# A load-bound log-sum-exp: an earlier Ln, one load fewer, and a first load issued as two partition halves from two queues

## The chip, the core and the metric

The kernel runs on one core of a Trainium2 chip. The time is device microseconds of that core, the median of several executions; single executions of the kernel before lie between 164.04 and 164.73 us over all sessions of this study.

## The reference

The input `x` has 32 x 512 rows of 1,024 float32 values (67.1 MB). The output is one float32 per row:

```python
x_max = np.max(x, axis=axis, keepdims=True)
return x_max.squeeze(axis) + np.log(np.sum(np.exp(x - x_max), axis=axis))
```

The kernel leaves out the maximum: it takes exp, sums, and takes the log. Each of the 128 SBUF partitions holds 128 rows.

## The kernel before

The 128 rows of each partition come in 18 loads ("chunks") into a ring of 51 row slots. ScalarE takes the exponential. In each chunk the first `n_dve` rows get one wide exponential and VectorE sums them; each other row gets an exponential of its own that also accumulates its sum. One Ln is taken early, over the rows of finished chunks, and one at the very end.

```python
CHUNKS = [   # (rows, rows summed by VectorE)
    (4, 0), (16, 10), (14, 13), (15, 4), (16, 7), (15, 6), (12, 9), (9, 6), (7, 5), (5, 4),
    (4, 3), (3, 3), (2, 2), (2, 0), (1, 1), (1, 0), (1, 0), (1, 0),
]
...
    def load(i):
        ...   # waits until the slots are free
        nc.sync.dma_start(out=ring[:, s : s + r], in_=x_v[:, row : row + r]).then_inc(
            landed[i], 16
        )
...
        if i == len(CHUNKS) - LN_EARLY:      # LN_EARLY = 6
            logged = place[i - 1][1]
            take_logs(0, logged, *done_before[i - 1])
        nc.scalar.wait_ge(landed[i], 16)
```

The first load is moved ahead of the barrier that opens the program, so that it is issued at 0.00 us of the profiled span. All loads are issued by SyncE and cover all 128 partitions.

The softmax here doesn't subtract the row's maximum and nothing guards it: scores larger than these inputs give would overflow.

Of the kernel before, what the change touches and what calls it, by code (L numbers as in the profile page):

```python
# [1 line left out]

# [4 lines left out]



CHUNKS = [  # L10
    (4, 0), (16, 10), (14, 13), (15, 4), (16, 7), (15, 6), (12, 9), (9, 6), (7, 5), (5, 4),
    (4, 3), (3, 3), (2, 2), (2, 0), (1, 1), (1, 0), (1, 0), (1, 0),
]
RING_ROWS = 51

LN_EARLY = 6


@with_exitstack
def kernel(  # L20
    ctx: ExitStack,
    tc: tile.TileContext,
    x: bass.AP,
    axis: bass.AP,
    out: bass.AP,
):
    nc = tc.nc
    P = nc.NUM_PARTITIONS

    assert axis in (-1, len(x.shape) - 1), f"only last-axis reduction supported, got {axis}"  # L30

    x_flat = x.flatten_outer_dims()
    N, D = x_flat.shape
    assert N % P == 0
    NB = N // P
    assert sum(r for r, _ in CHUNKS) == NB

    fp32 = mybir.dt.float32
    Exp = mybir.ActivationFunctionType.Exp
    Ln = mybir.ActivationFunctionType.Ln  # L40
    AX = mybir.AxisListType.X

    x_v = x_flat.rearrange("(p t) d -> p t d", p=P)
    out_v = bass.AP(tensor=out.tensor, offset=out.offset, ap=[[NB, P], [1, NB]])

    ring = nc.alloc_sbuf_tensor("ring", [P, RING_ROWS, D], fp32).ap()
    sums = nc.alloc_sbuf_tensor("sums", [P, NB], fp32).ap()
    res = nc.alloc_sbuf_tensor("res", [P, NB], fp32).ap()

    landed = [tc.alloc_semaphore(f"landed{i}") for i in range(len(CHUNKS))]  # L50
    act_done = tc.alloc_semaphore("act_done")
    dve_done = tc.alloc_semaphore("dve_done")
    stored = tc.alloc_semaphore("stored")


    hook = nc.pop_inst_callback()
    symbolic, nc._always_lower_symbolic_ap = nc._always_lower_symbolic_ap, False


    place = []  # L60
    row = slot = 0
    for r, _ in CHUNKS:
        if slot + r > RING_ROWS:
            slot = 0
        place.append((slot, row))
        slot += r
        row += r



    busy = [(0, 0)] * RING_ROWS
    acts = dves = 0

    def load(i):
        (s, row), r = place[i], CHUNKS[i][0]
        act_wait = max(a for a, _ in busy[s : s + r])
        dve_wait = max(d for _, d in busy[s : s + r])
        if dve_wait:
            nc.sync.wait_ge(dve_done, dve_wait)
        if act_wait:  # L80
            nc.sync.wait_ge(act_done, act_wait)
        nc.sync.dma_start(out=ring[:, s : s + r], in_=x_v[:, row : row + r]).then_inc(  # L82
            landed[i], 16
        )

    def take_logs(lo, hi, dve_wait, act_wait):
        nonlocal acts
        nc.scalar.wait_ge(act_done, act_wait)
        nc.scalar.wait_ge(dve_done, dve_wait)  # L89
        nc.scalar.activation(out=res[:, lo:hi], in_=sums[:, lo:hi], func=Ln).then_inc(  # L90
            act_done, 1
        )
        acts += 1

    body = nc.main_func.blocks[-1]
    assert not body.instructions
    load(0)
    n_early = len(body.instructions)

    nc.scalar.preload_act_table_set("natural_log_exp_and_others")  # L100

    logged = 0
    done_before = [(0, 0)]
    for i, (r, n_dve) in enumerate(CHUNKS):
        if i:
            load(i)
        s, row = place[i]
        if i == len(CHUNKS) - LN_EARLY:
            logged = place[i - 1][1]
            take_logs(0, logged, *done_before[i - 1])  # L110
        nc.scalar.wait_ge(landed[i], 16)
        if n_dve:
            nc.scalar.activation(  # L113
                out=ring[:, s : s + n_dve], in_=ring[:, s : s + n_dve], func=Exp
            ).then_inc(act_done, 1)
            acts += 1
            nc.vector.wait_ge(act_done, acts)
            nc.vector.reduce_sum(  # L118
                out=sums[:, row : row + n_dve], in_=ring[:, s : s + n_dve], axis=AX
            ).then_inc(dve_done, 1)  # L120
            dves += 1
            for j in range(n_dve):
                busy[s + j] = (0, dves)
        for j in range(n_dve, r):
            nc.scalar.activation(  # L125
                out=ring[:, s + j],
                in_=ring[:, s + j],
                func=Exp,
                accum_out=sums[:, row + j : row + j + 1],
            ).then_inc(act_done, 1)  # L130
            acts += 1
            busy[s + j] = (acts, 0)
        done_before.append((dves, acts))

    take_logs(logged, NB, dves, acts)
    nc.scalar.wait_ge(act_done, acts)
    nc.scalar.dma_start(out=out_v, in_=res).then_inc(stored, 16)
    nc.gpsimd.wait_ge(stored, 16)



    sp = mybir.EngineType.SP
    first = nc.main_func.blocks[0]
    head, work = first.instructions, body.instructions
    at = next(k for k, i in enumerate(head) if i.engine == sp and i.opcode == "Drain")
    end = next(k for k, i in enumerate(head) if i.opcode == "UnconditionalBranch")
    first.instructions = head[:at] + work[:n_early] + head[at:end] + work[n_early:] + head[end:]
    body.instructions = []

    nc._always_lower_symbolic_ap = symbolic  # L150
    nc.push_inst_callback(hook)


# [1 line left out]
_INS = ['x', 'axis']  # L155
_OUTS = [((32, 512), 'float32')]

_NUMBERS = {'axis': -1}


# [26 lines left out]
```

## Time and profile before

| | kernel before |
|---|---|
| time, median of 3 runs | 164.24 us (164.04 to 164.56) |
| span of the profiled execution | 162.7 us |
| load queue's share of the 16 DMA engines' time | 96.1% |
| ScalarE, VectorE busy | 76%, 49% |
| first chunk landed | 7.48 us |
| last chunk landed | 158.51 us |
| last exponential starts | 158.78 us |

The landings are read from the semaphore records: they show sixteen increments for a load, at separate times, and the sixteenth is the landing. The packet records give the start, duration and size of each piece that an engine moves; in the first load a packet is 16 KB, the four rows of one partition. They carry the queue but not the engine: where this text speaks of one engine's packets, each is taken to start where that engine's last one ended. The lines themselves stand in the prediction below, with what they show: the transfers never pause (the load queue fills 96.1% of the engines' time), and the end is the last landing at 158.51 us plus a short tail on ScalarE.

### The profile page before, as it was taken

How to read it: one execution, taken by the hardware profiler on the slowest of the kernel's cores; microseconds unless marked ns; L12 is line 12 of the kernel's file. 1: busy time of each engine (PE TensorE's matmuls, PEld its weight loads, DVE VectorE, ACT ScalarE, POOL GpSimd, SP SyncE). 2: the span in 40 equal slices, each digit the busy share in tenths (PEclk: the TensorE clock that was granted, in tenths of full speed). 3: DMA queues.
4: the chain of work that ended last, by engine and by line, in shares of the span. 5: the costliest groups of instructions: out<-in, count | busy, mean ns of one | idle time of the engine just before them, and what ended most of it. 6: DMA issues, size and time to landing. Idle time of an engine off the chain costs nothing.

```text
span 162.7 us, 208 instructions
## 1 busy us (share of the span) xinstructions
DVE 79.2 (49%) x13; ACT 123.2 (76%) x126; POOL 0.2 (0%) x4
## 2 busy tenths in 40 slices
DVE  0000000029940499990003940194009999999980
ACT  3180004999599707999099984999999999999893
POOL 0000000000000000000000000000000000000000
DMA  7997999989999979989997998998999999999960
GB/s 262 511 515 306 467 515 437 409 352 409 439 483 483 468 321 451 515 354 421 499 468 332 408 483 387 435 507 362 426 435 415 430 423 432 420 420 422 405 268 16
DMA packets 2737, 67.18 MB, mean 413 GB/s; under 512 B 304, under 2 KB 432, under 8 KB 944
## 3 DMA queue, kind: packets, MB, share of 16 engines
q1 hardware_dynamic: 2592, 67.11, 96.1%
q10 hardware_dynamic: 144, 0.07, 0.1%
q14 instruction: 1, 0.01, 0.0%
HBM read 67.11 MB, written 0.07 MB: 413 GB/s over the span
## 4 chain that ended last, share of the span: by engine, by line
DMA 45%; DVE 27%; ACT 26%; issue 0%; SPq 0%; ACTq 0%
DMA ring<-in_x_dram 45%; DVE sums L118 27%; ACT ring L113 17%; ACT ring L125 9%; ACT res L90 0%; SPq L82 0%; ACTq L89 0%
## 5 line engine op out<-in xcount | busy, mean ns | idle before, releaser
L118 DVE TENSOR_REDUCE sums<-ring 128x4 f32<-128x4096 f32 (+9 forms) x13 | 79.2, 6138 | 79.0 <-ACT ring L113 79.0
L113 ACT ACTIVATE ring<-ring 128x4096 f32<-128x4096 f32 (+9 forms) x13 | 64.8, 4987 | 30.3 <-DMA ring<-in_x_dram 30.2
L125 ACT ACTIVATE ring<-ring 128x1024 f32<-128x1024 f32 x55 | 57.2, 1040 | 5.5 <-DMA ring<-in_x_dram 5.5
L125 ACT ACTIVATION_READ_ACCUMULATOR ring<-ring 128x1 f32 x55 | 10.3, 187 | 0.0
L100 ACT ACT_TABLE_LOAD x1 | 1.3, 1283 | 0.8 <-PEq L168 0.8
L90 ACT ACTIVATE res<-sums 128x117 f32<-128x117 f32 (+1 forms) x2 | 0.5, 256 | 0.4 <-DVE sums L118 0.4
L168 POOL MEMSET const-bfloat16-1.0<- 128x1 bf16 x1 | 0.1, 102 | 0.0
L168 POOL MEMSET const-uint8-127<- 128x1 uint8 x1 | 0.1, 102 | 0.0
L168 POOL MEMSET const-float32-0.0<- 128x1 f32 x1 | 0.1, 99 | 0.2 <-issue 0.2
L168 POOL MEMSET const-float32-1.0<- 128x1 f32 x1 | 0.1, 99 | 0.0
## 6 DMA issues: line engine op xcount, KB each, us to landing
ring<-in_x_dram SPq DMA_DIRECT2D x2, 7680.0 KB, 45.3
ring<-in_x_dram SPq DMA_DIRECT2D x1, 7168.0 KB, 42.6
ring<-in_x_dram SPq DMA_DIRECT2D x1, 6144.0 KB, 40.9
ring<-in_x_dram SPq DMA_DIRECT2D x1, 4608.0 KB, 29.7
ring<-in_x_dram SPq DMA_DIRECT2D x2, 2048.0 KB, 20.0
ring<-in_x_dram SPq DMA_DIRECT2D x1, 3584.0 KB, 36.5
ring<-in_x_dram SPq DMA_DIRECT2D x1, 2560.0 KB, 28.1
ring<-in_x_dram SPq DMA_DIRECT2D x2, 1024.0 KB, 29.4
```

The lines of the kernel that those rows point to most:

```text
L90: nc.scalar.activation(out=res[:, lo:hi], in_=sums[:, lo:hi], func=Ln).then_inc(act_done, 1)
L100: nc.scalar.preload_act_table_set("natural_log_exp_and_others")
L113: nc.scalar.activation(out=ring[:, s : s + n_dve], in_=ring[:, s : s + n_dve], func=Exp).then_inc(act_done, 1)
L118: nc.vector.reduce_sum(out=sums[:, row : row + n_dve], in_=ring[:, s : s + n_dve], axis=AX).then_inc(dve_done, 1)
L125: nc.scalar.activation(out=ring[:, s + j], in_=ring[:, s + j], func=Exp, accum_out=sums[:, row + j : row + j + 1],).then_inc(act_done, 1)
L168: nc = _bacc.Bacc("TRN2", target_bir_lowering=False, num_devices=1)
```

## The change

The intent is to take the early Ln and its wait out of the tail, to save one load, and to have the DMA engines started sooner by handing the first load to two queues at once.

```diff
 CHUNKS = [
-    (4, 0), (16, 10), (14, 13), (15, 4), (16, 7), (15, 6), (12, 9), (9, 6), (7, 5), (5, 4),
-    (4, 3), (3, 3), (2, 2), (2, 0), (1, 1), (1, 0), (1, 0), (1, 0),
+    (4, 1), (15, 11), (16, 10), (16, 15), (16, 0), (14, 0), (12, 9), (9, 5), (7, 5), (5, 4),
+    (4, 3), (3, 0), (2, 2), (2, 2), (1, 0), (1, 0), (1, 0),
 ]
-LN_EARLY = 6
+LN_AT = 5
+FIRST_PARTS = [("sync", 0, 64), ("scalar", 64, 128)]
...
-        nc.sync.dma_start(out=ring[:, s : s + r], in_=x_v[:, row : row + r]).then_inc(
-            landed[i], 16
-        )
+        for engine, lo, hi in FIRST_PARTS if i == 0 else [("sync", 0, P)]:
+            getattr(nc, engine).dma_start(
+                out=ring[lo:hi, s : s + r], in_=x_v[lo:hi, row : row + r]
+            ).then_inc(landed[i], 16)
...
-        if i == len(CHUNKS) - LN_EARLY:
-            logged = place[i - 1][1]
-            take_logs(0, logged, *done_before[i - 1])
-        nc.scalar.wait_ge(landed[i], 16)
+        if i == LN_AT:
+            logged = row
+            take_logs(0, logged, *done_before[i])
+        nc.scalar.wait_ge(landed[i], 16 * (len(FIRST_PARTS) if i == 0 else 1))
```

The rest of the diff (cut) puts each early load ahead of its own engine's part of the opening barrier.

More of the change, by code (lines that the diff above doesn't have):

```diff
@@ L138 @@
     nc.gpsimd.wait_ge(stored, 16)
-    sp = mybir.EngineType.SP
     first = nc.main_func.blocks[0]
     head, work = first.instructions, body.instructions
-    at = next(k for k, i in enumerate(head) if i.engine == sp and i.opcode == "Drain")
     end = next(k for k, i in enumerate(head) if i.opcode == "UnconditionalBranch")
-    first.instructions = head[:at] + work[:n_early] + head[at:end] + work[n_early:] + head[end:]
+    head, tail = head[:end], head[end:]
+    for ins in work[:n_early]:
+        at = next(
+            k for k, i in enumerate(head) if i.engine == ins.engine and i.opcode == "Drain"
+        )
+        head.insert(at, ins)
+    first.instructions = head + work[n_early:] + tail
     body.instructions = []
```

## The prediction

Of the first rival, which the text goes on to call "a collision", only the size is left: each packet of a half load takes twice its 0.611 us, which makes +4.9 us and 169.

The 186 + 15 x 853 ns for an exponential of 15 rows agrees with the traces: 1,040 ns for one row and 11,296 for 13 in the kernel before make about 185 + 855 a row.

> **What bounds the kernel now.** I read the page first: the span, the DMA row of the 40 slices, the queue's share, and the chain that ended last.
>
> ```profile
> span 162.7 us, 208 instructions
> ...
> DMA  7997999989999979989997998998999999999960
> ...
> q1 hardware_dynamic: 2592, 67.11, 96.1%
> ...
> DMA 45%; DVE 27%; ACT 26%; issue 0%; SPq 0%; ACTq 0%
> ```
>
> The reader is to see that the one load queue fills 96.1% of the time of 16 DMA engines over the span, and that VectorE (49%) and ScalarE (76%) are not full. The chain names three causes in turn, but it follows buffer releases: the load queue always held the next load before the last one had landed (the fifth load was issued at 46.4 us while the fourth landed at 61.9). So the transfers never pause, and time is: start of the first packet, plus bytes at the engines' pace, plus what follows the last landing.
>
> The second view is the windows of the first microseconds (duration, DVE, ACT, POOL, clock, DMA share, GB/s).
>
> ```profile
> 1.00:1.50 0.50, 0.00 (x0) 0.50 (x1) 0.00 (x0) 1.00 0.70 164
> 1.50:2.00 0.50, 0.00 (x0) 0.50 (x1) 0.00 (x0) 1.00 1.01 295
> 2.00:2.50 0.50, 0.00 (x0) 0.06 (x1) 0.00 (x0) 1.00 0.62 262
> 2.50:3.00 0.50, 0.00 (x0) 0.00 (x0) 0.00 (x0) 1.00 1.07 459
> ```
>
> The load is issued at 0.0 and reaches its pace only after 2.5 us. The packet records beneath say why: the 16 engines take up their first packets between 1.00 and 2.01 us, and that first packet of 16 KB takes 0.61 to 1.51 us, where each later one takes 0.611. The engines end their eight packets at 6.35 to 7.12 us; without stagger and slow first packets it would be 1.00 + 8 x 0.611 = 5.9. The lag of one engine behind another then stays to the end, because each has the same bytes to move.
>
> The third view is the end: the windows of the DMA, and the timeline of ScalarE.
>
> ```profile
> 156.00:157.00 1.00, 1.00 (x2) 1.00 (x2) 0.00 (x0) 1.00 1.04 414
> 157.00:158.00 1.00, 1.00 (x2) 1.00 (x3) 0.00 (x0) 1.00 0.29 115
> 158.00:159.00 1.00, 0.15 (x1) 1.00 (x3) 0.00 (x0) 1.00 0.00 0
> ```
> ```profile
> 148.51 2.75 ACT L113 ACTIVATE ring<-ring 128x3072 f32<-128x3072 f32 x1
> 151.67 0.30 ACT L90 ACTIVATE res<-sums 128x117 f32<-128x117 f32 x1 [0.41 <-DVE sums L118]
> 151.88 1.89 ACT L113 ACTIVATE ring<-ring 128x2048 f32<-128x2048 f32 x1
> ...
> 156.70 1.04 ACT L125 ACTIVATE ring<-ring 128x1024 f32<-128x1024 f32 x1
> ...
> 157.74 1.04 ACT L125 ACTIVATE ring<-ring 128x1024 f32<-128x1024 f32 x1
> ...
> 158.78 1.04 ACT L125 ACTIVATE ring<-ring 128x1024 f32<-128x1024 f32 x1
> ...
> 159.94 0.21 ACT L90 ACTIVATE res<-sums 128x11 f32<-128x11 f32 x1
> 160.18 0.37 ACTq L137 DMA_DIRECT2D out_dram<-res  x1
> ```
>
> Data stop at 158.1; the last load's sixteen semaphore increments come from 157.40 to 158.51. The last exponential starts at 158.78, 0.27 after the last increment, because ScalarE runs without a gap from 151.67 on: it waited 0.41 us for VectorE before the early Ln and then spent some 0.2 on it. So the tail is bound by ScalarE, by a quarter of a microsecond.
>
> [...]
>
> **The change, part by part.**
>
> *17 loads.* From the packet records, by bytes per partition: 4 KB 161 ns, 60 KB 2267, 64 KB 2418, 56 KB 2116; eight of each per engine and load. The new list differs by one 64 KB load more, one 60 KB and one 4 KB load fewer: 8 x (2418 - 2267 - 161) = -80 ns, and a 9 ns semaphore write less: **-0.09 us** on the last landing.
>
> *Does the ring still feed the queue?* Rows 4 + 15 + 16 + 16 fill the 51 slots, so four loads go out at once, landing (pace 18.15 us per 15 rows, 19.35 per 16) at about 7.5, 25.6, 45.0 and 64.3. The tightest reload is the seventh, which needs VectorE's 15-row sum of the fourth chunk. The exponential starts at 64.3 and takes 186 + 15 x 853 ns = 13.0; the sum runs at 1.08 us per row (14.02 for 13 rows), 16.2. It ends at 93.5, while the sixth load lands at about 101. A margin of some 7 us; the fifth and sixth reloads have 17 and 19. ScalarE alone frees the later slots. No starvation: **0**.
>
> *Early Ln at the fifth chunk index.* It now logs 67 rows and needs the fourth chunk's sum (93.5), which is long done when ScalarE reaches it near 100.8 after 16 exponentials with accumulation (1.04 each). It costs about 0.3 us there, just as the sixth chunk lands, and later slack absorbs it. At the end both the 0.41 wait and the Ln are gone. I carried ScalarE's chain forward with pitches from the timeline (1.04 a row; 0.85 n + 0.09 for n rows) against landings shifted by the -0.09. It starts chunk seven at 115.65 (landed 115.60) and is never over 0.8 late; the longer 3-row chunk with accumulation, and two chunks of 2 rows, put the last exponential at about 158.6, against 158.78 before, just behind the landing at about 158.45. VectorE ends its last sum at 159.4, before the last Ln at 159.75. The last Ln has 61 columns instead of 11, +0.04. Net: **-0.15 us**, with the -0.09 inside it.
>
> *The first load in two halves.* SyncE and ScalarE each issue 64 partitions from 0.0 and about 0.1 us. ScalarE's arrival at the barrier comes after its own issue (0.37 us) and drain; the barrier was at 0.58, so it may be 0.1 later, harmless: the next load has until 6.3 us to be issued, and the table load (1.28 us) until the first landing. If the stagger of the first packets comes from feeding 128 descriptors through one queue, two half lists could cut it by up to half, 0.5 us. If it is the memory's first accesses, nothing. I take **-0.25 us**, and this is a choice, not a measurement; ScalarE's later starts move with the landings, so it would all reach the end.
>
> Sum: 164.24 - 0.15 - 0.25 = 163.84; I say **163.8**.
>
> **The rivals.**
> [...] the 2 MB would take 9.8 us instead of 4.9 (estimate: 8 packets x 0.611, doubled): +4.9 us, 169, slower by 3%. [...]
> *The start does not shorten.* [...] only -0.15 remains, 164.1.
> *ScalarE or VectorE takes over the end.* One of the chunks (3, 0), (2, 2), (2, 2) leaves a backlog. My margin for VectorE's last sum is 0.35 us. If it fails, the gain of the tail is lost: 164.0 to 164.4. Nothing could make it more, as the chain is full only by tenths.
> *An instruction fetch.* At 73.3 us an 8 KB fetch held one engine, which stays 0.43 behind the next one to the end. In the new kernel it may hit an engine with more or less lead: plus or minus 0.3.
>
> **Range and chances.** Without a collision I expect 163.2 to 164.3, from the start's 0 to -0.6 and the fetch. I give a collision of over a microsecond one chance in eight, which stretches the top: range 163.0 to 164.9. Faster by over 2% would need -3.3 us, where at most 1.2 is to be had at the start and 0.3 at the end: 0.01. Slower by over 2% needs most of the full collision: 0.07. The rest, 0.92, is within 2%.
>
> **What would show it.** Right: last landing at about 158.2, last exponential within 0.2 after it, no wait on VectorE before either Ln, load queue still near 96%, first packets of the engines begun within some 0.5 us, first chunk landed near 7.2 (or one big packet later, harmlessly, if an engine alternates with the second load). Wrong: 16 KB packets longer than 0.611 us after the ramp (the collision); an empty stretch of the DMA near 100 us (reload late); a wait for VectorE at the last Ln.

## The result

The changed kernel takes 169.75 us (median of 6 runs, 169.05 to 170.64), against 164.28 us for the kernel before in the same rounds. The ratio is 1.0337 (95% interval 1.0304 to 1.037). A ratio here is the mean time of one kernel's fast runs over that of the other's in the same rounds, so it is not quite the ratio of the two medians. The change made the kernel slower by 3.4%, and the time is outside the predicted range. The profiled execution of the changed kernel took 170.29 us, that of the kernel before 164.53; both are a little above their medians.

The page of the changed kernel, the same lines as in the prediction and the row of GB/s below the DMA row:

```profile
span 168.5 us, 214 instructions
...
DMA  8999699979997999699969999998999999999970
GB/s 187 260 354 339 292 467 467 467 342 436 498 451 311 482 498 451 296 498 498 451 296 436 438 436 436 502 420 385 440 429 429 417 436 397 428 425 419 412 311 16
...
q1 hardware_dynamic: 2384, 66.06, 93.7%
q10 hardware_dynamic: 224, 1.11, 2.8%
```

The row of GB/s of the kernel before:

```profile
GB/s 262 511 515 306 467 515 437 409 352 409 439 483 483 468 321 451 515 354 421 499 468 332 408 483 387 435 507 362 426 435 415 430 423 432 420 420 422 405 268 16
```

The DMA row does not tell that anything is wrong: the engines are as busy as before (the queues' lines sum to 96.5% of their time, to 96.2% before). The GB/s row does. A slice is about 4.2 us; the first five slices carry 187, 260, 354, 339 and 292 where the kernel before had 262, 511, 515, 306 and 467. (Large packets are counted where they start, so single slices jump up and down: before, 1,131 GB/s from 6 to 7 us and none from 10 to 11. Only sums over several mean something.) From the sixth slice on both are at the same pace. Two windows make it sharper; the columns are the window, its length, DVE, ACT and POOL busy, clock, DMA busy share, GB/s. Kernel before:

```profile
2.50:4.50 2.00, 0.00 (x0) 0.00 (x0) 0.00 (x0) 1.00 1.02 434
```

Changed kernel:

```profile
2.50:4.50 2.00, 0.00 (x0) 0.26 (x1) 0.00 (x0) 1.00 1.09 246
11.00:15.00 4.00, 0.00 (x0) 0.00 (x0) 0.00 (x0) 1.00 1.03 311
```

With the DMA share at 1.02 to 1.09 in all three, the changed kernel moves 246 GB/s in place of 434 in the middle of its first load, and still 311 when the second load is under way. The packet records agree: the median of the 16 KB packets that start between 2.8 and 4.5 us is 0.611 us before and 1.27 us after. The first half of the first chunk has landed at 8.72 us and the second at 20.68, where the whole chunk was in at 7.48 before.

Where the 5.8 us of the span come from can be added up. I sum, over the packets of the first load, what each took beyond 0.611 us, and divide by 16 engines: 0.40 us per engine before, 4.33 after, so +3.9. I do the same for the 60 KB packets of the second load, whose usual time is 2.267 us: 48 of them, three for each engine, took 2.4 to 3.6 us, which is +2.0 per engine; no packet of the second load before (64 KB, usually 2.418) took more than 2.47. That makes +6.0. The measured last landing is 164.41 in place of 158.51, +5.90.

The tail got shorter, as intended:

```profile
164.53 1.04 ACT L128 ACTIVATE ring<-ring 128x1024 f32<-128x1024 f32 x1
165.48 0.19 ACT L128 ACTIVATION_READ_ACCUMULATOR ring<-ring 128x1 f32 x1
165.69 0.25 ACT L93 ACTIVATE res<-sums 128x61 f32<-128x61 f32 x1
165.98 0.36 ACTq L140 DMA_DIRECT2D out_dram<-res  x1
```

These are ScalarE's last lines in the timeline of the changed kernel. The last exponential starts 0.12 us after the last landing, where it was 0.27 before.

### The profile page after: what moved, and what is told of

Same layout as the page of the kernel before. It is cut to its first block, busy times and chain, and to the rows that moved or that the text cites. A ratio compares the mean times of both kernels' runs of the same rounds, so it can differ in the third digit from the quotient of the medians.

```text
span 168.5 us, 214 instructions
## 1 busy us (share of the span) xinstructions
DVE 72.9 (43%) x11; ACT 124.0 (74%) x136; POOL 0.2 (0%) x4
## 4 chain that ended last, share of the span: by engine, by line
ACT 50%; DMA 40%; DVE 7%; issue 1%
DMA ring<-in_x_dram 40%; ACT ring L128 28%; ACT ring L116 21%; DVE sums L121 7%; ACT res L93 0%
## 5 line engine op out<-in xcount | busy, mean ns | idle before, releaser
L121 DVE TENSOR_REDUCE sums<-ring 128x5 f32<-128x5120 f32 (+8 forms) x11 | 72.9, 6648 | 92.3 <-ACT ring L116 92.2
L116 ACT ACTIVATE ring<-ring 128x5120 f32<-128x5120 f32 (+8 forms) x11 | 59.3, 5393 | 35.1 <-DMA ring<-in_x_dram 35.1
L128 ACT ACTIVATE ring<-ring 128x1024 f32<-128x1024 f32 x61 | 63.4, 1040 | 5.3 <-DMA ring<-in_x_dram 5.3
L128 ACT ACTIVATION_READ_ACCUMULATOR ring<-ring 128x1 f32 x61 | 11.4, 187 | 0.0
L93 ACT ACTIVATE res<-sums 128x67 f32<-128x67 f32 (+1 forms) x2 | 0.5, 256 | 0.1
```

The lines of the kernel that those rows point to most:

```text
L93: nc.scalar.activation(out=res[:, lo:hi], in_=sums[:, lo:hi], func=Ln).then_inc(act_done, 1)
L116: nc.scalar.activation(out=ring[:, s : s + n_dve], in_=ring[:, s : s + n_dve], func=Exp).then_inc(act_done, 1)
L121: nc.vector.reduce_sum(out=sums[:, row : row + n_dve], in_=ring[:, s : s + n_dve], axis=AX).then_inc(dve_done, 1)
L128: nc.scalar.activation(out=ring[:, s + j], in_=ring[:, s + j], func=Exp, accum_out=sums[:, row + j : row + j + 1],).then_inc(act_done, 1)
```

## The experiments

**The theories.** The partition theory: what counts is the set of partitions that a transfer writes; one that covers partitions 0 to 63 alone (or 64 to 127 alone) keeps all 16 DMA engines busy, but each of its packets takes about twice as long, as in the changed kernel (1.27 us for 0.611). In the expectations what stands after "[...]" is what this theory expects. Rival A: the chunk list or the place of the Ln costs the time. Rival B: the second queue costs, by taking turns or by its issue. Rival C: any transfer of fewer than 128 partitions is slow. Rival D: it is the half of the input in memory that is read, not what is written.

Eight kernels were run. The runs of the kernel before had a median of 164.57 us in the session of the first four and 164.21 us in that of the other four.

### The first load whole again

```diff
-FIRST_PARTS = [("sync", 0, 64), ("scalar", 64, 128)]
+FIRST_PARTS = [("sync", 0, 128)]
```

> Changed kernel with one edit: the first load goes out whole (128 partitions, SyncE) again; the new chunk list and the Ln at index 5 stay. [...] the whole loss is gone, 16 KB packets are back at 0.611 us, last landing near 158.4, time 163.9 to 164.2, just under the kernel before. Rival A (the new chunk list or the early Ln costs the time): stays near 169.7.

Measured: 164.28 us, ratio 0.9985 (0.9973 to 0.9998). The same window reads:

```profile
2.50:4.50 2.00, 0.00 (x0) 0.00 (x0) 0.00 (x0) 1.00 0.99 418
```

The median 16 KB packet is back at 0.611 us, and the last landing at 158.58. The whole loss sits in the split; rival A falls. What is left of the change is a gain of about a quarter of a microsecond.

### The split alone, in the kernel before

The kernel before with `FIRST_PARTS` as in the change; chunk list and Ln are the old ones.

> Kernel before with the split of the first load alone (old chunk list, old place of the Ln). [...] 16 KB packets of 1.27 us, first chunk landed near 20 us, about 6 us more than before: 170.0 to 170.5. Rival A: near 164.3.

Measured: 170.33 us, ratio 1.0357 (1.032 to 1.0394), first chunk landed at 22.11 us, median packet 1.28 us.

```profile
2.50:4.50 2.00, 0.00 (x0) 0.26 (x1) 0.00 (x0) 1.00 1.11 238
```

The split alone brings the loss; its interval overlaps that of the whole change (1.0304 to 1.037).

### Both halves on one queue

```diff
-FIRST_PARTS = [("sync", 0, 64), ("scalar", 64, 128)]
+FIRST_PARTS = [("sync", 0, 64), ("sync", 64, 128)]
```

> Changed kernel, but both halves are issued by SyncE, one after the other. [...] all eight 16 KB packets of each engine still take 1.27 us (8 x 0.66 more, less some 0.7 of slow ramp that is there in any case: +4.6), but the second load's big packets come after them and stay at 2.27, so a little less is lost than with two queues: 168 to 169. Rival B (turn-taking between two queues, or ScalarE's own issue, is what costs): 164.

Measured: 169.37 us, ratio 1.029 (1.0275 to 1.0305).

```profile
2.50:4.50 2.00, 0.00 (x0) 0.61 (x1) 0.00 (x0) 1.00 1.10 229
11.00:15.00 4.00, 1.22 (x1) 2.57 (x4) 0.00 (x0) 1.00 1.06 430
```

One half at a time, from one queue, also moves at 229 GB/s; two queues are not needed for the loss. By 11 us the engines are at full pace again, where two queues held the changed kernel at 311. The first chunk is in at 12.41 us. The last landing is 163.05, 1.36 earlier than with two queues. That compares one of the shorter executions of this kernel (168.95 us, median 169.37) with one of the longer ones of the changed kernel (170.29, median 169.75); by the ratios, which come from different rounds, the second queue costs about 0.8 us (1.0337 against 1.029), and the two intervals just touch. The time is 0.4 above the range; the records show what the expectation left out: one 60 KB packet of most engines was still slow, 0.5 us per engine. Rival B does not explain the loss, but the second queue seems to add to it: the 60 KB packets lost 2.0 us per engine with it and 0.5 without.

### Halved by rows instead of partitions

```diff
-FIRST_PARTS = [("sync", 0, 64), ("scalar", 64, 128)]
+FIRST_PARTS = [("sync", 0, 2), ("scalar", 2, 4)]
...
-                out=ring[lo:hi, s : s + r], in_=x_v[lo:hi, row : row + r]
+                out=ring[:, s + lo : s + hi], in_=x_v[:, row + lo : row + hi]
```

Two queues, both ahead of the barrier, but each transfer covers all 128 partitions.

> Changed kernel, but the first load is halved by rows instead of partitions: SyncE loads rows 0 and 1, ScalarE rows 2 and 3, each for all 128 partitions, both ahead of the barrier. [...] no packet is slowed (8 KB packets at 0.31 us), time 163.5 to 164.3; if two queues do shorten the ramp it is at the low end and below the run with the whole load. Rival B (two queues cost): 167 to 170.

Measured: 164.22 us, ratio 0.9982 (0.9968 to 0.9995).

```profile
2.50:4.50 2.00, 0.00 (x0) 0.00 (x0) 0.00 (x0) 1.00 1.02 426
11.00:15.00 4.00, 0.00 (x0) 0.89 (x1) 0.00 (x0) 1.00 1.08 467
```

Two queues cost nothing that shows when each transfer covers all 128 partitions, even though the ScalarE part took turns with the second load and was in only at 14.09 us. They also gain nothing that can be told from the whole load (0.9982 against 0.9985). The engines' first packets started within 0.5 us instead of 1.0, as hoped for, but the first load's packets of an engine took 0.50 us beyond their usual time against 0.52 for the whole load, and the last landing is the same (158.55 against 158.58). So a second queue does not cure the slow start; what makes it slow was not shown.

These records also show when the turns begin, which bears on the prediction: every engine took four of SyncE's eight packets before the first of ScalarE's (at 2.75 to 3.25 us), and only then one of each in turn, although the two parts were issued within 0.13 us. Why four, no record shows.

### The middle 64 partitions first

```diff
-FIRST_PARTS = [("sync", 0, 64), ("scalar", 64, 128)]
+FIRST_PARTS = [("sync", 32, 96), ("sync", 0, 32), ("sync", 96, 128)]
```

> Changed kernel, first load in three pieces on SyncE: partitions 32 to 96, then 0 to 32, then 96 to 128. [...] the first four 16 KB packets of each engine take 0.61 us after the ramp, the other four 1.27 us, and the time is about 2.6 us over the run with the whole load: 166.5 to 167.3. Rival C (any transfer of fewer than 128 partitions is slow, whichever they are): all eight packets take 1.27 us, 169 or more.

That the middle partitions would be fast and the two outer pieces slow was not shown by any run before this one.

Measured: 167.13 us, ratio 1.0175 (1.0161 to 1.0188).

```profile
2.50:4.50 2.00, 0.00 (x0) 0.86 (x1) 0.00 (x0) 1.00 1.00 418
5.50:7.50 2.00, 0.00 (x0) 0.00 (x0) 0.00 (x0) 1.00 0.93 205
```

This is the clearest run. Partitions 32 to 95 are 64 partitions too, and they move at 418 GB/s; partitions 0 to 31 and then 96 to 127, right after, at 205. The packets of one engine in the packet records, one after the other, took 1.162, 0.611, 0.627 and 0.618 us, then 0.705, about 1.26, 1.19 and so on; those that start from 7.5 us on, all of partitions 96 to 127 by their order, have a median of 1.20. Rival C falls: it is which partitions are written together, not how many (64 of them at 418 GB/s here, 64 at 229 with the halves on one queue). What the 16 KB packets took beyond 0.611 us is 2.59 us per engine, about half of the 4.80 of both halves on one queue, as half the bytes are slow; the cost in time against the kernel before is 2.9 us, against 4.8.

### The same, read from other rows

```diff
+FIRST_PARTS = [("sync", 32, 96, 0, 64), ("sync", 0, 32, 64, 96), ("sync", 96, 128, 96, 128)]
...
-                out=ring[lo:hi, s : s + r], in_=x_v[lo:hi, row : row + r]
+                out=ring[lo:hi, s : s + r], in_=x_v[slo:shi, row : row + r]
```

> As the run before, but the piece that is written to partitions 32 to 96 is read from the rows that belong to partitions 0 to 64, and the next piece from those of 64 to 96: the result is wrong on purpose, the bytes are the same in number. [...] nothing changes against the run before, since only the partitions written count (first four packets 0.61 us). Rival D (the half of the input in memory that is read makes it slow): the first four packets take 1.27 us.

Measured: 167.14 us (one run, state unknown).

```profile
2.50:4.50 2.00, 0.00 (x0) 0.87 (x1) 0.00 (x0) 1.00 0.93 393
```

The median 16 KB packet that starts between 2.8 and 4.5 us took 0.611 us. The rows of partitions 0 to 63, slow when written to partitions 0 to 63, are fast when written to 32 to 95. Rival D falls. (Four rows of 96 partitions end in a wrong place, and the comparison with the reference passed all the same: the log-sums of 1,024 normal draws differ by little, a standard deviation of 0.04 around 7.43 in the reference's values, worked out from the input.)

### The early Ln alone

The kernel before, with `LN_AT = 5` and the new rule for what is logged; first load whole, old list.

> Kernel before, first load whole, old list of 18 loads, only the early Ln moved to index 5. My reading of the tail: the 0.41 us wait for VectorE and the 0.2 us Ln leave ScalarE's last stretch, so its last exponential starts within 0.1 us of the last landing; 0.2 to 0.25 us less than before, ratio 0.9985. Rival: the Ln in mid-stream delays a reload and nothing is gained, ratio 1.000.

Measured: 164.01 us, ratio 0.9985 (0.9972 to 0.9999).

```profile
153.20 1.06 ACT L128 ACTIVATE ring<-ring 128x1024 f32<-128x1024 f32 x1 [0.40 <-DMA ring<-in_x_dram]
...
158.32 1.04 ACT L128 ACTIVATE ring<-ring 128x1024 f32<-128x1024 f32 x1
```

ScalarE now waits 0.40 us for a load near the end, which it never did before: the tail is bound by the landings. The last exponential starts 0.05 us after the last landing (158.27).

### The new list alone

First load whole, new list of 17 loads, the Ln six loads before the end as it was.

> First load whole, new list of 17 loads, the early Ln at its old place six loads before the end. Reading: the last landing comes 0.09 us earlier by the packet sums, but ScalarE's late Ln still delays the last exponential; gain under 0.2 us, ratio 0.999 to 1.001. Rival (the list is what gains): ratio 0.9985, as with both parts.

Measured: 164.33 us, ratio 0.9999 (0.9986 to 1.0013).

```profile
149.24 0.28 ACT L93 ACTIVATE res<-sums 128x114 f32<-128x114 f32 x1
...
158.22 1.04 ACT L128 ACTIVATE ring<-ring 128x1024 f32<-128x1024 f32 x1
```

There is no wait for VectorE before the Ln here, but the last exponential again trails the last landing (157.97) by 0.25 us. The list alone gains nothing that five rounds can show; the small gain seems to belong to the place of the Ln (0.9985), though the intervals of the two runs overlap.

No experiment gave a version clearly faster than the kernel before. The whole first load with the other two parts (0.9985), the row halves (0.9982) and the early Ln alone (0.9985) are all ahead of it by 0.25 to 0.3 us, with intervals just below 1; they also beat the changed kernel.

## Why the prediction was wrong, point by point

- **What bounds the kernel:** right. What held the DMA engines up at the start reached the end in full: 5.90 us at the last landing of the profiled execution, from a stretch that was over by 21 us.
- **"The first load in two halves: -0.25 us":** this is the step that failed. It measured about +5.9 us (ratio 1.0357 when done alone, of 164.57), because the packets of the two halves took 1.26 and 1.16 us (medians of all 64 of each half, changed kernel) in place of 0.611. The choice rested on a shorter start, which the row halves show not to exist: first packets closer together, same last landing.
- **The collision, one chance in eight:** this was the true course, and its sign, 16 KB packets longer than 0.611 us, came. The prediction named the size for packets of twice the time, +4.9 us and 169, and then set it aside; its range ended at 164.9. It set it aside with two arguments that rested on no trace. The first was that the two halves would be in work at the same time, taken in turns by the engines. The packet records of the changed kernel show otherwise: the last 16 KB packet of SyncE's half started at 5.38 us, the first of ScalarE's on any engine at 5.59. So the engines were all on the low half together, then on the high half, from about 8 us on in turns with the second load. The row halves show the same order: turns begin only after four of SyncE's packets, and a half of partitions has just four for each engine. The second argument was that each half might fall on eight engines. But while SyncE's half alone was under way, from 2.5 to 5 us, 16 packets were in flight at a time, all of its queue, at a DMA share of about 1.1; at 6.8 us all 16 were of ScalarE's; and each half shows sixteen increments, at separate times, from 7.87 to 8.72 us and from 18.24 to 20.68. So each half used all 16 engines. That 169 lies so near the measured 169.75 is in part luck: the 16 KB packets cost +3.9 us, not +4.9, and the rest came from a term that the prediction did not have.
- **The term that was missing:** "one big packet later, harmlessly". Each engine took turns between ScalarE's packets and the 60 KB packets of the second load, and those 60 KB packets were slowed as well, +2.0 us per engine. With one queue they lose 0.5 us; with row halves, which also take turns, 0.06. So the full size takes both, transfers of half the partitions and two queues. Why the 60 KB packets slow down in these turns, no record shows; that part is open.
- **Early Ln and list, -0.15 us:** right in kind, with a size above the forecast; the three runs with the Ln moved and no partition halves measured 0.9982 to 0.9985, which is 0.25 to 0.3 us, where the intervals reach from almost nothing to 0.5. The list's share, put at -0.09, can't be told from nothing (0.9999).
- **Ring and reloads:** right. The seventh load, the tightest by the prediction, was issued at 99.95 us in the changed kernel, while the load before it landed at 107.00. The DMA share is 0.99 and 0.96 in the windows from 98 to 104 and from 104 to 110 us, at 430 and 415 GB/s.
- **The barrier "0.1 later, harmless":** it came 0.7 later (1.40 instead of 0.70 us; the prediction's 0.58 is the barrier's first record), since ScalarE's half took 0.55 us to issue, as did SyncE's (the whole load before: 0.37), and the drain after it, which stands before the barrier, 0.53. The row halves took 0.38 and 0.15, and their barrier came 0.14 later; so this goes with the partition pieces. It was harmless for the next load. The earliest packet also started at 1.33 us instead of 1.00, but the mean of the 16 engines' first starts is 1.53 us in both kernels, so no cost shows in that.

How far the partition theory is shown: the runs show that the rate depends on the set of partitions written. It is 434 GB/s for 0 to 127 and 418 for 32 to 95. For the low half it is 229 to 246 (16 engines with packets of 16 KB in 1.27 us make 206, worked out), for the low quarter 205; for the high half and the high quarter the packets took 1.16 and 1.20 us in place of 0.611. That it is low for a half does not depend on the second queue (229 GB/s on one), nor that it is high for 32 to 95 on the rows read (393 with other rows). Why these sets are slow and the middle one is not, no record shows.

## What to carry to other kernels

Give every bulk load all 128 partitions, and if it has to be cut, cut it along the free dimension (the rows within a partition): the row halves moved at 426 GB/s here and cost nothing that shows (ratio 0.9982), while a half made of partitions 0 to 63 moved at 229 to 246, from one queue and from two (1.029 and 1.0337). The partition split cost about 6 us, on a 2 MB load that took 6.1 us when whole (first packet at 1.00, last ended at 7.12). When DMA is the bound, read the GB/s beside the busy share: a packet that is slowed counted as busy for all its time, so the share stayed near 1.0 while the rate fell from 434 to 246. And where a rival course has a worked-out size, 169 us here, let the range reach it unless a measured number speaks against it; no such number did.
